# The first layer's output projection: seven block products in both pairs of columns, row sums on GpSimd

## The chip, the cores and the metric

One core of one Trainium2 chip runs the whole program. The metric is device microseconds of one execution, the median of three runs. The profile is of one more execution, whose own time and span are given below. PE is TensorE (PEld its weight load), DVE is VectorE, ACT is ScalarE, POOL is GpSimd, SP is SyncE.

## The reference

A trunk of two residual layers on 512 tokens of width 2048, all in fp32: layer 0 is gated differential attention, layer 1 is RWKV-7 time mixing. The change lies in the last product of layer 0:

```python
    out = lax.map(one_block, (jnp.arange(nb), qb))        # per head: a = p0 - lam * p1; a @ v
    ...
    o = rms_norm(o, subln_w) * (1.0 - lambda_init)
    o = o.reshape(B, T, DA_WIDTH).astype(h.dtype) * jax.nn.silu(gate)
    return o @ w_out                                      # (512, 2048) @ (2048, 2048)
...
        x = x + out.astype(x.dtype)
```

Its left operand is made head by head (8 heads of 256 columns), so its last 256 rows of K exist only when the last head's attention is done.

## The kernel before, in words

**Products.** An fp32 product is made of three matmuls of rounded halves: each operand is split into a high part and a low part, and hi x hi, hi x lo and lo x hi are added in PSUM (mm3, L123). The left operand of the output projection is the transposed result of attention, kept as 16 K tiles of 128 rows; each is a pair of tiles hH and hL of 128 x 512. The right operand is the weight, loaded 512 KB at a time (two K tiles of 512 columns) into a tile; `split_w` (L92) rounds it to wh on ACT (L105) and subtracts on DVE to get wl (L106). There are two buffers each of wh and wl.

**The projection's two units.** The output has four column blocks of 512. Blocks 0 and 1 are made one after the other by `unit_tok` (L167): 8 weight tiles for each block, 24 matmuls of 128 x 512 for each tile, summed in four PSUM banks; then DVE adds the residual x (L1100), and the result is squared on ACT (L1078) and stored. Blocks 2 and 3 are made together by `seven` (L750) in the manner of Strassen: tokens, K tiles and columns are halved, and seven block products replace eight. Sums of weight blocks are made in memory by DMAs that accumulate (`add_w`, L83), issued by POOL into the same tile that holds the first block (ropeC, ropeS, T and others). Sums of blocks of the left operand are made by `sum_forms` (L669): DVE adds hH and hL into a row buffer `frow` (L678), DVE makes the four forms S1, S3, S2, S4 in place (L687), ACT rounds each to its high half (L699), DVE subtracts for the low half (L700). With NS = 6, 12 of the 16 K tiles go through block products (three groups of 2 + 2 K tiles) and 4 K tiles (12 to 15) are plain. A weight tile in a block product feeds 12 matmuls, in a plain step 24.

**What goes beside it.** While blocks 0 and 1 are made, the attention of the last head still runs: a chain of steps (scores, exps on ACT, transposes, weighted sums, y) is stepped after every so many matmuls of the projection (`Chain`; the number is the gap, here 20, after a delay of 16). The chain for the last head writes its result straight into rows 14 and 15. For each of its four blocks of 128 queries DVE has the masked maximum (L345), the difference of the two softmax parts (L359), the low half of the transposed weights (L369), a reciprocal root by small steps (L64 to L71), y (L384) and the low halves of the transposed y (L418).

**What sets the order.** The kernel is written with tiles and priorities, and a scheduler fixes each engine's instruction order when the program is built; an engine runs its list in that order, and waits at an instruction whose input or buffer is not ready. `issue_after` adds an edge to another instruction, `high_priority` moves instructions forward in the list (splits by AHEAD, the taking of PSUM sums by SCAN). The rows of the earlier heads come from memory, where they were stored; SP loads them as hH and hL (L1055), 28 loads of 256 KB, issued up to 725.3 us.

Of the kernel before, what the change touches and what calls it, by code (L numbers as in the profile page):

```python
# [668 lines left out]
def sum_forms(g, src, i, rows, homes, halves, behind=None):  # L669
# [4 lines left out]
    for r, k0 in zip(rows, (half[i] for half in halves)):  # L674
        if isinstance(src, list):
            for k in range(KG):
                with g.tc.issue_after(g.rowsplit):
                    nc.vector.tensor_add(r[:, k], *(x[:].bitcast(F32) for x in src[k0 + k]))  # L678
# [4 lines left out]
    out = {}
    for nm, o, x, y, op in (("S1", d, b, d, ALU.subtract), ("S3", b, a, b, ALU.subtract),
                            ("S2", d, d, a, ALU.subtract), ("S4", c, c, d, ALU.add)):
        with g.tc.issue_after(behind or g.rowsplit):
            nc.vector.tensor_tensor(out=o, in0=x, in1=y, op=op)  # L687
# [201 lines left out]
def loader(g, w, homes):  # L889
# [3 lines left out]
    def load(k0, c):  # L893
# [3 lines left out]
        g.fetched = load_w(g, raw, (w, c), k0, slice(0, KG))  # L897
# [12 lines left out]
def layer0(g, aps):  # L910
    nc, tc = g.nc, g.tc
    with ExitStack() as cx:
# [137 lines left out]
        rows = []  # L1050
        for k in range(KT - 2):
            rows.append([g.hp.tile([P, T], F32R, name=n, tag=n) for n in ("hH", "hL")])
            for x, d in zip(rows[k], g.ys):
                with tc.issue_after(g.reloaded):
                    loaded = nc.sync.dma_start(out=x[:].bitcast(F32), in_=d[k * P : (k + 1) * P, :]).ins  # L1055
        ch = Chain(g, attention(g, h, *before, 20, rows, rest), 16)

        def all_rows(n, _):
            if n >= KT - 1:
                ch.finish(g)  # L1060

        yH, yL = Rows(rows, 0), Rows(rows, 1)
        g.ssx = g.const.tile([P, NT, 4], F32, name="ssx")
        g.hH, g.hL, xs = [], [], []

        def new_x(cb):
# [5 lines left out]
            return xq  # L1072
# [898 lines left out]
```

## Time and profile before

| what | number |
|---|---|
| median of 3 runs | 2050.31 us (2050.27 to 2052.22) |
| the profiled execution | 2051.32 us, its span 2049.6 us |
| granted TensorE clock | 1.000 |
| PE, DVE, ACT, POOL busy in the span | 2032.6, 1626.3, 1139.3, 409.4 us |
| output projection's first matmul | 714.15 us |
| first accumulating DMA in it (POOL) | 810.95 us |
| stretch 714.1 to 766.9 us | PE busy 52.59 of 52.80, DVE 39.12, ACT 23.83, POOL 0 |

The page gives busy time by engine, then the span in 40 slices, the DMA queues, the chain that ended last, the costliest groups of instructions. Rows of groups read: line, engine, operation, out<-in, shape, count, busy time and mean duration (ns), idle time before and what ended it. Rows of windows read: window, its length, busy time and count of PE, PEld, DVE, ACT, POOL, granted clock, DMA share, GB/s. Rows of the timeline read: start, length, engine, line, operation. Rows of waits read: who waited, for whom, microseconds in all, times, longest.

### The profile page before, as it was taken

To read this page: it belongs to the slowest core of one execution; us is meant where nothing else is said; L and a number is where in the kernel's file an instruction comes from. 1 tells how busy PE (TensorE), PEld (TensorE's weight loads), DVE (VectorE), ACT (ScalarE), POOL (GpSimd) and SP (SyncE) were. 2 spreads that over 40 slices of the span, in tenths; PEclk is the share of its full clock that TensorE was granted. 3 is DMA by queue.
4 is the path that set the end of the run, shared out by engine and by line. 5 is a ranking of instruction groups with operands and counts; after the bars stand their busy time and mean duration, and the time that the engine had idled before them with its cause. 6 is when DMAs were issued, how large, how long until landed. Compare 5 with 4: busy or idle time off the path is not lost. (4 is left out here: it accounts for less than half of the span.)

```text
span 2049.6 us, 34167 instructions
## 1 busy us (share of the span) xinstructions
PE 2032.6 (99%) x11898; PEld 1668.7 (81%) x11898; DVE 1626.3 (79%) x4126; ACT 1139.3 (56%) x2264; POOL 409.4 (20%) x786
## 2 busy tenths in 40 slices
PE   9999999999999999999999999999999999999999
PEld 8888888888888888888877788888888888877787
DVE  7988988888898977575787888877778878778865
ACT  5765656565666544355565555555555555546433
POOL 1020111102011000121122322222232222232211
PEclk9999999999999999999999999999999999999999
DMA  8487978879787965723323323233333332346796
GB/s 288 156 165 193 180 173 184 165 193 165 190 180 171 270 218 176 174 93 108 103 79 92 93 82 96 83 101 98 98 98 88 95 88 88 101 137 217 178 270 142
DMA packets 160845, 300.90 MB, mean 147 GB/s; under 512 B 64560, under 2 KB 81968, under 8 KB 160672
## 3 DMA queue, kind: packets, MB, share of 16 engines
q1 hardware_dynamic: 110416, 183.34, 28.4%
q0 software_dynamic: 26528, 92.98, 23.9%
q10 hardware_dynamic: 23728, 22.40, 3.4%
q8 instruction: 94, 1.54, 0.3%
q14 instruction: 79, 0.65, 0.1%
HBM read 274.48 MB, written 24.18 MB: 146 GB/s over the span
## 5 line engine op out<-in xcount | busy, mean ns | idle before, releaser
L106 DVE TENSOR_TENSOR wl<-wraw,wh 128x1024 fp32r<-128x1024 f32 (+1 forms) x284 | 347.5, 1224 | 155.2 <-ACT wh L105 146.1
L105 ACT CAST wh<-wraw 128x1024 fp32r<-128x1024 f32 (+1 forms) x284 | 297.4, 1047 | 232.2 <-PE pp L125 102.8
L125 PE MATMUL pp<-hL,wh 128*128 128x512 f32 x1024 | 413.5, 404 | 0.0
L125 PE MATMUL pp<-hH,wl 128*128 128x512 f32 x1024 | 413.1, 403 | 0.0
L125 PE MATMUL pp<-hH,wh 128*128 128x512 f32 x1024 | 412.3, 403 | 0.1
L125 PEld LDWEIGHTS pp<-hH,wh 128*128 128x128 f32 x1024 | 193.1, 189 | 34.5 <-ACT wh L105 0.4
L125 PEld LDWEIGHTS pp<-hL,wh 128*128 128x128 f32 x1024 | 193.1, 189 | 33.6
L125 PEld LDWEIGHTS pp<-hH,wl 128*128 128x128 f32 x1024 | 193.2, 189 | 32.5
L572 PE MATMUL pp<-wh,hH 128*128 128x512 f32 x448 | 176.8, 395 | 0.0
L572 PE MATMUL pp<-wh,hL 128*128 128x512 f32 x448 | 175.8, 393 | 0.0
L1516 DVE SCALAR_TENSOR_TENSOR tmpl<-LT,Tm 128x60 f32<-128x60 f32 (+24 forms) x496 | 135.0, 272 | 13.3
L1660 POOL COPY SA<-VS 64x64 f32<-64x64 f32 x224 | 59.4, 265 | 405.4 <-DVE VS L1676 367.4
L572 PE MATMUL pp<-wl,hH 128*128 128x512 f32 x448 | 140.2, 392 | 0.0
L125 PE MATMUL pp<-wl,hH 128*128 128x512 f32 x340 | 133.7, 393 | 0.0
L125 PE MATMUL pp<-wh,hH 128*128 128x512 f32 x340 | 133.3, 392 | 0.1
L125 PE MATMUL pp<-wh,hL 128*128 128x512 f32 x340 | 133.0, 391 | 0.1
L1518 DVE TENSOR_TENSOR Tm<-Tm,tmpl 128x60 f32<-128x60 f32 (+24 forms) x496 | 103.6, 209 | 11.7
L1657 ACT COPY rhs<-sm 64x64 f32<-64x64 f32 x256 | 53.1, 207 | 83.7 <-PE sm L1654 80.7
L572 PEld LDWEIGHTS pp<-wl,hH 128*128 128x128 f32 x448 | 84.4, 188 | 17.3
L572 PEld LDWEIGHTS pp<-wh,hH 128*128 128x128 f32 x448 | 84.2, 188 | 17.5 <-issue 0.4
L572 PEld LDWEIGHTS pp<-wh,hL 128*128 128x128 f32 x448 | 84.2, 188 | 16.0
L1667 ACT COPY VS<-sm 64x64 f32<-64x64 f32 x256 | 52.9, 206 | 75.2 <-PE sm L1665 69.2
(433 smaller groups left out, 4438.4 us busy)
## 6 DMA issues: line engine op xcount, KB each, us to landing
wraw<-in_rw_w_in_dram SPq DMA_DIRECT2D x128, 512.0 KB
wraw<-in_da_w_in_dram SPq DMA_DIRECT2D x75, 512.0 KB
wraw<-in_da_w_in_dram POOLq DMA_DIRECT2D x28, 512.0 KB, 6.6
wraw<-in_da_w_out_dram SPq DMA_DIRECT2D x26, 512.0 KB
Ta<-in_da_w_in_dram POOLq DMA_DIRECT2D x21, 512.0 KB, 5.5
Tb<-in_da_w_in_dram POOLq DMA_DIRECT2D x21, 512.0 KB, 5.7
Tc<-in_da_w_in_dram POOLq DMA_DIRECT2D x21, 512.0 KB, 5.3
Td<-in_da_w_in_dram POOLq DMA_DIRECT2D x21, 512.0 KB, 5.6
```

The lines of the kernel that those rows point to most:

```text
L105: a = nc.scalar.copy(hi[:, ks], raw[:, ks])
L106: d = nc.vector.tensor_sub(lo[:, ks], raw[:, ks], hi[:, ks].bitcast(F32))
L125: m = nc.tensor.matmul(out, a, b, start=s, stop=e, skip_group_check=skip)
L572: m = nc.tensor.matmul(out[t][:], x, wt[lo][:, k, :], start=first, stop=end and lo == 1 and k == KG - 1, skip_group_check=True)
L1516: nc.vector.scalar_tensor_tensor(tt, LT[:, i : i + 1, i + 1 :].to_broadcast([P, s, n]), n2[:, i : i + 1], Tm[:, 0:s, i : i + 1].to_broadca ...
L1518: nc.vector.tensor_add(Tm[:, 0:s, i + 1 :], Tm[:, 0:s, i + 1 :], tt)
L1657: nc.scalar.copy(rhs[r_, :], sm[r_, h * C : h * C + C])
L1660: nc.gpsimd.tensor_copy(p.SA[r_, c - 1, :], VS[r_, c, h, :])
L1667: g.copied = nc.scalar.copy(VS[r_, c, h, :], sm[r_, P : P + C])
```

## The change

Blocks 0 and 1 are now made together too, by `seven_early`, a function that the kernel already has (L812) and uses for layer 1's output projection. One step works on one weight tile. Its steps: 1 to 3 plain, K tiles 4, 10 and 12 (each with the next) for column block 0; 4 and 5 plain, 4 and 10 for block 1; then the block products on two groups of 2 + 2 K tiles (0 and 6, 2 and 8): 6 and 7 (the block called 11), 8 and 9 (12), 10 and 11 (the form S1); 12 plain; 13 and 14 (S2), 15 and 16 (S4), 17 plain, 18 and 19 (S3), 20 plain, 21 and 22 (block 22). K tiles 14 and 15, the last head's, are in the plain steps 17 and 20. Blocks 2 and 3 are made by `seven` with all 16 K tiles in block products, four groups. 

Row sums and forms are made by GpSimd (`nc.gpsimd` as `adder`), for four groups where there were three, one group's forms at a time at the steps that the table `at` names; the halves are still split by ACT and DVE. The forms' order is S1, S2, S4, S3 (also in layer 1's projection, where DVE still makes them). The rows are loaded in another order (4, 5, 10 to 13 first, then the residual of block 0, then 0, 1, 6, 7, the residual of block 1, then 2, 3, 8, 9), the weights of the first unit with the priority AHEAD, and the gap of the last head's chain is 24.

```diff
+FORMS = "S1", "S2", "S4", "S3"
+
+
+def sum_forms(g, src, i, rows, homes, halves, behind=None, names=FORMS, adder=None):
 
 
 
     nc = g.nc
...
-                with g.tc.issue_after(g.rowsplit):
-                    nc.vector.tensor_add(r[:, k], *(x[:].bitcast(F32) for x in src[k0 + k]))
+                with g.tc.issue_after(behind or g.rowsplit):
+                    (adder or nc.vector).tensor_tensor(out=r[:, k], in0=src[k0 + k][0][:].bitcast(F32),
+                                                       in1=src[k0 + k][1][:].bitcast(F32), op=ALU.add)
...
-    for nm, o, x, y, op in (("S1", d, b, d, ALU.subtract), ("S3", b, a, b, ALU.subtract),
-                            ("S2", d, d, a, ALU.subtract), ("S4", c, c, d, ALU.add)):
+    for nm, o, x, y, op in (("S1", d, b, d, ALU.subtract), ("S2", d, d, a, ALU.subtract),
+                            ("S4", c, c, d, ALU.add), ("S3", b, a, b, ALU.subtract)):
+        if nm not in names:
+            continue
         with g.tc.issue_after(behind or g.rowsplit):
-            nc.vector.tensor_tensor(out=o, in0=x, in1=y, op=op)
+            (adder or nc.vector).tensor_tensor(out=o, in0=x, in1=y, op=op)
...
-        rows = []
-        for k in range(KT - 2):
-            rows.append([g.hp.tile([P, T], F32R, name=n, tag=n) for n in ("hH", "hL")])
-            for x, d in zip(rows[k], g.ys):
-                with tc.issue_after(g.reloaded):
-                    loaded = nc.sync.dma_start(out=x[:].bitcast(F32), in_=d[k * P : (k + 1) * P, :]).ins
-        ch = Chain(g, attention(g, h, *before, 20, rows, rest), 16)
-
-        def all_rows(n, _):
-            if n >= KT - 1:
-                ch.finish(g)
-
-        yH, yL = Rows(rows, 0), Rows(rows, 1)
-        g.ssx = g.const.tile([P, NT, 4], F32, name="ssx")
-        g.hH, g.hL, xs = [], [], []
+        rows = [None] * (KT - 2)
+        halves = [0, 2, 4, 12], [6, 8, 10, 14]
+        first = [k for k0 in (4, 10, 12) for k in (k0, k0 + 1)]
+        others = [0, 1, 6, 7, 2, 3, 8, 9]
+        for k in others + first:
+            rows[k] = [g.hp.tile([P, T], F32R, name=n, tag=n) for n in ("hH", "hL")]
+        xs = []
...
+        for some, cb in ((first, 0), (others[:4], 1), (others[4:], None)):
+            for k in some:
+                for x, d in zip(rows[k], g.ys):
+                    with tc.issue_after(g.reloaded):
+                        loaded = nc.sync.dma_start(out=x[:].bitcast(F32), in_=d[k * P : (k + 1) * P, :]).ins
+            if cb is not None:
+                new_x(cb)
+        g.rowsplit = loaded
+        ch = Chain(g, attention(g, h, *before, 24, rows, rest), 16)
+
...
-        for cb in range(2):
-            pts = unit_tok(g, yH, yL, (aps["da_w_out"], cb), 512, more=(all_rows, all_sums)[cb],
-                           late=cb == 0)
-            xq = new_x(cb)
-            for t in range(NT):
-                nc.vector.tensor_add(xq[:, t, :], xq[:, t, :], pts[t][:])
-                store_x(cb, t)
...
+        at = dict(zip((1, 2, 4, 6, 8, 9, 11, 12, 13, 15, 16, 17, 18, 19, 20, 21),
+                      [(i, nm) for k in (0, 2) for nm in FORMS for i in (k, k + 1)]))
+
+        def between(n):
+            if n == 14:
+                ch.finish(g)
+            if n in at:
+                i, nm = at[n]
+                if i == len(sums):
+                    sums.append({})
+                    frow = g.work.tile([P, 2, KG, 512], F32, name="frow", tag=("sB2", "sC2", "qkT", "qkL")[i], bufs=1)
+                    frows.append([frow[:, x] for x in range(2)])
+                sums[i].update(sum_forms(g, rows, i, frows[i], homes, halves, g.m.ins, nm, nc.gpsimd))
+
...
+        load = loader(g, aps["da_w_out"], [(g.wraw, "wraw", 3)], AHEAD)
+        seven_early(g, aps["da_w_out"], load, rows, sums, 0, 1, residual(0), [flat(g.S), T2[:]], banks, stores(0),
+                    [x[:2] for x in halves], (4, 10, 12), 14, between)
...
-        seven(g, aps["da_w_out"], load, rows, sums, 2, 3, acc, [flat(g.C), flat(g.S), T2], banks, done, begin)
+        for cb in (2, 3):
+            new_x(cb)
+        T3 = g.work.tile([P, KG, 512], F32, name="T3", tag="Te", bufs=1)
+        seven(g, aps["da_w_out"], load, rows, sums, 2, 3, residual(2), [flat(g.C), T3[:], flat(g.S), T2[:]], banks,
+              stores(2), begin, halves)
```

GpSimd's list at the projection, before. The rows after the last head's weight adds are the second unit's accumulating DMAs (ropeC, ropeS and T are the tiles that hold the weight blocks):

```order
113 L86 DMA wraw<-in_da_w_in_dram 128x1024 x3
114 L86 DMA ropeC<-in_da_w_out_dram 128x1024
115 L86 DMA ropeS<-in_da_w_out_dram 128x1024
116 L86 DMA T_8533<-in_da_w_out_dram 128x1024
117 L86 DMA ropeC<-in_da_w_out_dram 128x1024
```

And now, at the same place (L680 the row sums, L692 the forms, T_7653 the tile T2):

```order
113 L86 DMA wraw<-in_da_w_in_dram 128x1024 x3
114 L680 TENSOR_TENSOR frow<-hH,hL 128x512 x4
115 L692 TENSOR_TENSOR frow<-frow 128x2x256 x4
116 L680 TENSOR_TENSOR frow<-hH,hL 128x512 x4
117 L692 TENSOR_TENSOR frow<-frow 128x2x256 x4
118 L86 DMA ropeS<-in_da_w_out_dram 128x1024
119 L680 TENSOR_TENSOR frow<-hH,hL 128x512 x5
120 L692 TENSOR_TENSOR frow<-frow 128x2x256
121 L680 TENSOR_TENSOR frow<-hH,hL 128x512
122 L692 TENSOR_TENSOR frow<-frow 128x2x256
123 L86 DMA T_7653<-in_da_w_out_dram 128x1024
```

The sums of the first two groups stand ahead of the first accumulating DMA, and eight sums of the third group stand between that DMA and the next.

ACT's list in the second block of the last head's attention, before (L368 the high half of the transposed weights, L351 the exps, L105 the fifth weight tile's cast):

```order
697 L368 CAST at<-pt 128x128
698 L351 ACTIVATE a,sm<-sc,nb,sq 128x256
699 L351 ACTIVATE sc,sm<-sc,nb,sq 128x256
700 L105 CAST wh<-wraw 128x1024
701 L378 ACTIVATE o,so<-o,r 128x256
```

And now, where L707 are the casts of GpSimd's forms:

```order
697 L707 CAST fS_7694<-frow 128x512
698 L707 CAST fS_8255<-frow 128x512
699 L368 CAST at<-pt 128x128
700 L707 CAST fS_7926<-frow 128x512
701 L707 CAST fS_8183<-frow 128x512
702 L105 CAST wh<-wraw 128x1024
703 L351 ACTIVATE a,sm<-sc,nb,sq 128x256
704 L351 ACTIVATE sc,sm<-sc,nb,sq 128x256
```

Two casts of the first group stand ahead of the transposed weights, two more ahead of the fifth weight tile's cast.

DVE's list around step 7 (the split of tile T2, L106), which has in it the accumulations into the residual (L748), the low halves of forms (L708) and attention's steps:

```order
1669 L748 TENSOR_TENSOR xq<-xq,pp 128x512
1670 L69 SCALAR_TENSOR_TENSOR rs_t<-rs_t,so 128x1
1671 L348 SCALAR_TENSOR_TENSOR nb<-mx,sq 128x1
1672 L106 TENSOR_TENSOR wl<-T_7653,wh 128x1024
1673 L71 SCALAR_TENSOR_TENSOR ro<-rs_t,rs_i 128x1
1674 L708 TENSOR_TENSOR fS_8206<-frow,fS_8205 128x512
1675 L382 SCALAR_TENSOR_TENSOR ro<-ro,r,stats_107 128x1
1676 L708 TENSOR_TENSOR fS_8522<-frow,fS_8522 128x512
1677 L384 SCALAR_TENSOR_TENSOR y<-o,ro,G 128x256
```

Before, no L678, L687 or L700 row of this projection and no accumulation into the residual stood among attention's rows.

More of the change, by code (lines that the diff above doesn't have):

```diff
@@ L747, in pieces, with seven @@
     return prod, plain, take
-def seven(g, w, load, rows, sums, c1, c2, acc, Ts, banks, done, begin=None, halves=evenly(NS)):
+def seven(g, w, load, rows, sums, c1, c2, acc, Ts, banks, done, begin=None, halves=None):
     prod, plain_, take = pieces(g, load, rows, sums, acc, halves)
@@ L896, in load @@
         raw = pool.tile([P, KG, 512], F32, name="wraw", tag=tag, bufs=bufs)
-        g.fetched = load_w(g, raw, (w, c), k0, slice(0, KG))
+        with g.tc.high_priority(offset=offset):
+            g.fetched = load_w(g, raw, (w, c), k0, slice(0, KG))
         return raw
@@ L1071, in new_x @@
             xs.append(xq)
-            return xq
+        for some, cb in ((first, 0), (others[:4], 1), (others[4:], None)):
[7 more added lines that the diff above has]
+        ch = Chain(g, attention(g, h, *before, 24, rows, rest), 16)
+        g.ssx = g.const.tile([P, NT, 4], F32, name="ssx")
+        g.hH, g.hL = [], []
         def store_x(cb, t):
@@ L1083, in layer0 @@
                              for t in tags]
-        homes = ({"S1": one("dd0H", "dd0L"), "S2": one("VL"), "S4": one("t1", "t1"), "S3": one("t1", "t1")},
-                 {"S1": one("Td"), "S2": one("sA2"), "S4": one("acc1"), "S3": one("Ta")},
-                 {"S1": one("at", "al"), "S2": one("sC2"), "S4": one("dd1H", "dd1L"),
-                  "S3": one("Tc")})
-        def all_sums(n, _):
-            if n >= 4 * len(sums) + 2 and len(sums) < NS // KG:
-                frow = g.work.tile([P, 2, KG, 512], F32, name="frow", tag=("qkT", "qkL")[len(sums) % 2],
-                                   bufs=1)
-                sums.append(sum_forms(g, rows, len(sums), [frow[:, i] for i in range(2)], homes, evenly(NS)))
@@ L1095, in layer0 @@
[L1095 to L1108 removed]
+        halved = {}
@@ new lines, in half_of, with home @@
+        def half_of(tag):
+            def home():
+                if tag not in halved:
+                    both = g.work.tile([P, 2, 2, KG, 256], F32R, name="f" + tag, tag=tag, bufs=1)
+                    halved[tag] = [both[:, 0], both[:, 1]]
+                return halved[tag].pop(0)
+            return home
+        homes = ({"S1": one("dd0H", "dd0L"), "S2": one("Ta"), "S4": one("acc1"), "S3": one("dd1H", "dd1L")},
+                 {"S1": one("Td"), "S2": half_of("sA2"), "S4": one("t1", "t1"), "S3": one("t1", "t1")},
+                 {"S1": one("at", "al"), "S2": one("VL"), "S4": half_of("sC2"), "S3": one("Tc")},
+                 {"S1": half_of("sA2"), "S2": half_of("sB2"), "S4": half_of("sB2"), "S3": half_of("sC2")})
@@ L1110, in banks, with residual, stores, done @@
+        def residual(c0):
+            return {nm: [xs[c0 + c][:, 2 * t + i, :] for i in range(2)] for nm, (t, c) in PLACES.items()}
+        def stores(c0):
+            def done(nm):
+                t, c = PLACES[nm]
+                for i in range(2):
+                    store_x(c0 + c, 2 * t + i)
+            return done
         def banks(i):
```

22 lines of the change are left out of this document (8 added, 14 removed).

## The prediction

> **What bounds the kernel now.** I read the head of the page first, then the stretch of the output projection (714 to 893 us of the span) in windows, then its waits, its groups of instructions, and single rows of the timeline.
>
> ```profile
> PE 2032.6 (99%) x11898; PEld 1668.7 (81%) x11898; DVE 1626.3 (79%) x4126; ACT 1139.3 (56%) x2264; POOL 409.4 (20%) x786
> ```
> ```profile
> 740.00:750.00 10.00, 9.93 (x55) 7.91 (x53) 8.24 (x33) 5.67 (x14) 0.00 (x0) 1.00 0.43 155
> 750.00:760.00 10.00, 9.88 (x54) 8.04 (x52) 6.40 (x30) 4.75 (x11) 0.00 (x0) 1.00 0.33 99
> 770.00:780.00 10.00, 10.00 (x46) 8.29 (x45) 9.93 (x15) 6.62 (x15) 0.00 (x0) 1.00 0.57 187
> 780.00:790.00 10.00, 10.00 (x45) 8.29 (x45) 9.92 (x16) 4.24 (x6) 0.00 (x0) 1.00 0.37 123
> 860.00:870.00 10.00, 10.00 (x46) 8.29 (x45) 5.80 (x6) 4.04 (x4) 3.20 (x4) 1.00 1.05 195
> ```
> The columns are length, busy time of PE, PEld, DVE, ACT and POOL, granted clock, DMA share, GB/s. PE is the bound: no gap, full clock. So matmuls that go are gained, unless something else then arrives late. DVE is almost full at 770 to 790, where it makes the row sums, but that is no bound: PE beside it has no gap. What one matmul is worth is read from start to start, not from its busy time (0.39 us, overlapped with the next):
>
> ```profile
> 870.28 0.39 PE L125 MATMUL pp<-wh,fS 128*128 128x512 f32 x1
> 870.50 0.39 PE L125 MATMUL z<-wh,hH 128*128 128x512 f32 x1
> 870.73 0.39 PE L125 MATMUL z<-wl,hH 128*128 128x512 f32 x1
> 870.96 0.39 PE L125 MATMUL z<-wh,hL 128*128 128x512 f32 x1
> ```
> That is 0.227 us each (0.68 us for three). Last, who waits there:
>
> ```profile
> POOL ropeC L86 <- DVE wl L106: 156.6, 3, 133.8
> ACT wh L105 <- PE pp L125: 45.3, 26, 4.4
> DVE wl L106 <- ACT wh L105: 41.4, 26, 4.2
> PE z L125 <- DVE wl L106: 0.2, 1, 0.2
> ```
> POOL does nothing for 133.8 us up to its first accumulating DMA; ACT and DVE wait for buffers that PE frees, up to 4.4 us. PE's own longest wait is 0.2 us.
>
> **The change, part by part.** *Matmuls.* A plain pair of columns costs 384 matmuls (16 K tiles, 4 row tiles, 2 columns, 3 each). Each pair of K tiles in block products saves 6. Before: 384 for the first unit, 384 - 6x6 = 348 for the second. Now 384 - 4x6 = 360 and 384 - 8x6 = 336. So 732 become 696: 36 fewer, 36 x 0.227 = **8.2 us gained** if nothing is late.
>
> *DVE.* It loses the row sums and forms, and gains splits and accumulations:
>
> ```profile
> L687 DVE TENSOR_TENSOR frow<-frow 128x512 f32<-128x512 f32 x12 | 8.3, 688 | 0.1
> L678 DVE TENSOR_TENSOR frow<-hH,hL 128x512 f32<-128x512 f32 x12 | 7.7, 686 | 0.0
> L700 DVE TENSOR_TENSOR fS<-frow,fS 128x512 fp32r<-128x512 f32 x12 | 8.1, 687 | 0.7 <-ACT fS L699 0.7
> L699 ACT CAST fS<-frow 128x512 fp32r<-128x512 f32 x12 | 7.1, 618 | 9.1 <-DVE frow L687 9.0
> L1100 DVE TENSOR_TENSOR xq<-xq,pp 128x512 f32<-128x512 f32 x8 | 5.1, 684 | 1.2 <-PE pp L125 1.2
> L106 DVE TENSOR_TENSOR wl<-wraw,wh 128x1024 fp32r<-128x1024 f32 x33 | 40.4, 1224 | 23.3 <-ACT wh L105 23.2
> L105 ACT CAST wh<-wraw 128x1024 fp32r<-128x1024 f32 x33 | 34.7, 1052 | 35.9 <-PE pp L125 27.8 <-DVE xq L745 4.4 <-PE pp L572 1.6
> ```
> Gone: 24 x 0.687 = 16.5 us. Added: 4 more low halves (2.7 us), and the accumulations into the residual, 28 + 16 where there were 8 + 20, so 16 x 0.684 = 10.9 us. Over the projection DVE is 2.9 us lighter, which is worth nothing in itself. What counts is the place. Before, all of it came after attention, at 764 to 830. Now accumulations and low halves stand between the steps of the last head's attention, on the same in-order DVE, and from step 6 each weight tile feeds 12 matmuls (2.7 us) instead of 24 (5.4 us), so splits come twice as often. Each tile's split (L106) must be done before PE may begin its step.
>
> ```profile
> 735.36 1.23 DVE L106 TENSOR_TENSOR wl<-wraw,wh 128x1024 fp32r<-128x1024 f32 x1
> ```
> ```profile
> 736.50:766.89 30.39, 30.19 (x152) 24.42 (x151) 23.20 (x93) 12.58 (x29) 0.00 (x0) 1.00 0.48 166
> ```
> ```profile
> L106 DVE TENSOR_TENSOR wl<-wraw,wh 128x1024 fp32r<-128x1024 f32 x5 | 6.1, 1224 | 0.0
> L678 DVE TENSOR_TENSOR frow<-hH,hL 128x512 f32<-128x512 f32 x3 | 2.0, 684 | 0.0
> L379 DVE TENSOR_SCALAR so<-so 128x1 f32<-128x1 f32 x4 | 0.6, 150 | 3.4 <-ACT o L378 3.4
> L355 DVE RECIPROCAL r<-sm 128x2 f32<-128x2 f32 x2 | 0.3, 161 | 1.0 <-ACT sc L351 1.0
> ```
> The split of the fifth tile ends at about 736.5. In the 30.4 us behind it DVE is busy 23.2, of which 6.1 and 2.0 are splits and row adds (the first two rows below it, of the same window): 15.1 us are attention's. In the new order there stand, behind the fifth split up to and with that of step 11: 6 splits (7.3 us), 8 accumulations (5.5), 7 low halves (4.8) and some 15 us of attention, together 32.6. So the split of step 11 ends at 736.5 + 32.6 = 769.1 at the earliest. When does PE want it? Ahead of step 11 stand 5 x 24 + 5 x 12 = 180 matmuls of the projection:
>
> ```profile
> 714.10:766.90 52.80, 43.81 (x180) 32.88 (x180) 0.69 (x1) 0.00 (x0) 1.00 0.69 233
> ```
> ```profile
> 748.69 0.36 PE L125 MATMUL o<-V,at 128*128 128x256 f32 x1
> 748.88 0.28 PE L125 MATMUL o<-VL,at 128*128 128x256 f32 x1
> ```
> The first row is the projection's matmuls alone: PE had issued 180 by 766.9. In the new order 12 narrow ones of attention (0.19 apart by the other two rows) and four transposes (about 0.1 each, an estimate) come only later, so PE would be there at about 764.2. DVE makes it 769.1 - 764.2 = **4.9 us late**, and PE cannot win that back. Some of DVE's waits stay as well: behind 736.5 it waits 3.4 us for attention's squares (L379) and 1.0 for the exps now; work that fills most of that gap leaves me 0.8 us (my choice between 0 and 4.4).
>
> *GpSimd's adds.* Of a two-input add there no row exists. Nearest rows:
>
> ```profile
> L1568 POOL COPY G<-AR 64x512 f32<-64x512 f32 x24 | 17.2, 715 | 93.1 <-PE px L1561 92.4
> L1480 POOL TENSOR_SCALAR_AFFINE_SELECT G<-G 64x1024 f32<-64x1024 f32 x32 | 37.2, 1161 | 1.0
> ```
> ```profile
> 882.53 8.48 POOL L1126 TENSOR_SCALAR xq<-xq,rs 128x512 f32<-128x512 f32 x4 [13.74 <-DVE rs L71]
> 900.30 6.46 POOL L1126 TENSOR_SCALAR xq<-xq,rs 128x512 f32<-128x512 f32 x4 [9.30 <-DVE rs L71]
> ```
> A copy of 512 elements takes 0.72 us, a pass over 1024 takes 1.16, a multiplication of 512 by a row's scale 1.6 to 2.1. An add reads twice 512, so I take 1.2, with 0.72 and 2.12 as ends. [...] No run here shows it yet.
>
> Two places hang on it. First: the four row adds and four forms of the first group need rows that are loaded last but for four.
>
> ```profile
> 725.26 0.38 SPq L1055 DMA_DIRECT2D hL<-ys  x1
> ```
> ```profile
> 720.00:730.00 10.00, 9.98 (x50) 7.99 (x50) 6.84 (x24) 5.66 (x14) 0.00 (x0) 1.00 0.99 337
> 745.71 0.39 PE L125 MATMUL sc<-qkT,qkL 128*128 128x512 f32 x1
> ```
> The loads of rows are issued up to 725.3 with the DMA full (0.99), and I put the first group's last row at 728 (an estimate). One row add and four forms follow: 728 + 5 x 1.2 = 734. The last cast (0.62) then stands ahead of the fifth tile's cast (1.05) on ACT and its split (1.22): 736.9, against 736.5. Nothing. Second: the third group's buffer is that of the last head's q and k, free after PE's last scores: 745.7 before, and some 1.5 later now, since DVE's first lateness falls ahead of it. Eight GpSimd instructions lie between that and the form S3 of that group, whose cast (ACT) and low half (DVE) stand ahead of attention's and of the splits of steps 8 to 11: 747.2 + 9.6 + 0.6 = 757.4, where DVE by its own sum comes at 755.9. That is **1.5 us**. At 0.72 it is nothing; at 2.12 the first place costs 5 and the second 9.
>
> *DMA.* The accumulating loads go from 12 to 24, 16 of them in the second unit.
>
> ```profile
> q0 software_dynamic: 1728, 6.29, 38.7%
> q1 hardware_dynamic: 1749, 5.41, 17.9%
> ```
> From 800 to 893 us: 12 adds of 512 KB took 38.7% of 93 us, 3.0 us of all engines each; a plain load 1.6. The second unit (336 x 0.227 = 76 us) asks for 16 x 3.0 + 12 x 1.6 = 67 us, with stores and residual some 13 more: just full. An add has at least one round of four tiles (10.9 us) to land. I take 0.5 us, between 0 and 4.
>
> *Same cost before and after*: reordered row loads and the other order of the forms in layer 1's projection (nothing late there: PE is full).
>
> **Sum**: -8.2 + 4.9 + 0.8 + 1.5 + 0.5 = **-0.5 us** on the profiled execution, 2051.3 (span 2049.6 and 1.7 around it). That one lies 1.0 above the median of 2050.3, so the forecast is 2050.8 there and 2049.8 for a median.
>
> **Rivals.** *All is hidden.* DVE's extra work in attention fits into its gaps, GpSimd's into its idle time. For it: PE waits for nobody now, DVE idles 7.2 of 30.4 us, POOL altogether. Against it: 32.6 us of DVE rows in some 28. It gives -8.2: 2042.
>
> *The GpSimd adds decide (slower).* At 1.7 us the fifth tile's cast comes 2.9 us late, the third group's S3 another 5.5: -8.2 + 4.9 + 0.8 + 2.9 + 5.5 + 0.5 = +6.4, 2056.7. It decides from about 1.55 us. For it: the multiplication rows; against it: the pass over 1024.
>
> *DVE and GpSimd keep each other out (slower).* While DVE was busy 9.32 of 10 us the four multiplications took 8.48 us, later 6.46: something makes GpSimd slower beside a busy DVE.
>
> ```profile
> 880.00:890.00 10.00, 9.82 (x43) 7.76 (x42) 9.32 (x17) 5.74 (x9) 7.47 (x4) 1.00 0.31 113
> ```
> DVE's own splits kept 1.22 us. If each of the 13 low halves and splits behind 736.5 had to wait out half an add (0.6), DVE would be 7.8 us later: +7.3, 2057. [...]
>
> *The second unit is bound by its adds.* The queue of 80 us of transfers in 76 costs 4 us instead of 0.5: +3, 2053. For it 1.05 in the window at 860 with three tiles a round; against it, PE has no gap there.
>
> **How the numbers follow.** Chances: forecast 0.39, all hidden 0.25, slow adds 0.18, keeping out 0.07, adds in the second unit 0.11. A measurement of this kernel can tell about 0.2%, 4.1 us. Faster by more: all hidden, and a tenth of the forecast's, 0.29. Same: most of the forecast, two thirds of the last rival, a little of the slow adds, 0.43. Slower: the rest, 0.28. The forecast's own range is 2046.5 to 2053 (add at 0.72, to 1.4 us). The range that holds 8 in 10 reaches from all hidden to slow adds: 2041.5 to 2057.5.
>
> **What would show it.** Matmuls of the projection: 696, and the end of the projection moved by less than 8.2 us. GpSimd's add rows near 1.2 us. In the windows from 740 to 775, DVE over 9.5 of 10, and PE gaps there of some 7 us in all, ended by splits (L106) that end late; before 736 none. In the second unit hardly a gap. I am wrong if DVE has idle time in that stretch, if PE's gaps name casts of GpSimd's forms from step 4 on, or if PE has no gaps.

## The result and the profile after

The changed kernel is slower: 2071.64 us (median; 2068.87 to 2073.44) against 2051.26 us (2050.27 to 2052.77) for the kernel before on the same chip, a ratio of 1.0093 with an interval of 1.0078 to 1.0108. The forecast was 2049.8, its range ended at 2057.5. The profiled execution, the longest of the four, has a span of 2071.7 us where the kernel before had 2049.6: 22.1 us to be found.

Where are they? The mark I use is GpSimd's first causal mask in layer 1, which both kernels come to 60 us after the projection. Of its six instructions the group's row names the start of the first; the first row is of the kernel before, the second of the changed one.

```profile
L1478 POOL TENSOR_SCALAR_AFFINE_SELECT G<-G x6: 654/656/690, 953.7 to 1066.7; 64x512 f32<-64x512 f32 x6
```
```profile
L1509 POOL TENSOR_SCALAR_AFFINE_SELECT G<-G x6: 653/654/658, 968.6 to 1080.9; 64x512 f32<-64x512 f32 x6
```

So 14.9 us are lost by then, 7.2 later. The projection's own end moved by the same 14.9: the first matmul behind it (`lora`) starts at 908.6 us, before at 893.7. The head of the page, then the four largest of PE's waits between 720 and 910 us, then windows of 10 us there:

```profile
PE 2035.1 (98%) x11862; PEld 1669.1 (81%) x11862; DVE 1651.6 (80%) x4131; ACT 1151.1 (56%) x2277; POOL 468.3 (23%) x830
```
```profile
PE pt L365 <- DVE rs_i L65: 5.6, 1, 5.6
PE pp L125 <- DVE wl L106: 3.4, 1, 3.4
PE pt L297 <- ACT t L282: 2.5, 1, 2.5
PE z L125 <- DVE wl L106: 2.3, 2, 1.7
```
```profile
720.00:730.00 10.00, 7.54 (x31) 5.89 (x30) 7.20 (x20) 3.94 (x11) 4.94 (x4) 0.83 0.92 319
740.00:750.00 10.00, 4.38 (x17) 3.73 (x16) 9.39 (x20) 2.81 (x9) 7.98 (x6) 0.86 0.69 255
760.00:770.00 10.00, 6.02 (x23) 4.32 (x23) 10.00 (x17) 3.12 (x6) 9.97 (x8) 0.88 0.07 13
800.00:810.00 10.00, 8.30 (x28) 5.85 (x27) 8.81 (x8) 5.44 (x7) 7.17 (x6) 0.83 0.74 147
860.00:870.00 10.00, 10.00 (x46) 8.29 (x45) 5.73 (x6) 3.74 (x4) 3.21 (x4) 1.00 1.06 202
```

The matmuls are gone as counted: 11862 against 11898, 36 fewer. But PE, whose longest wait in the projection before was 0.2 us, now has four long ones in the first unit. All eight rows of that view add to 16.2 us. And the granted clock is below 1 there: the windows from 720 to 810 that lie below 1 lack 0.17, 0.14, 0.03, 0.12, 0.05 and 0.17, times 10 us makes 6.8 us. So -8.2 + 16.2 + 6.8 = 14.8, against 14.9 measured. (The sum is that good in part by luck: two of the slow stretches begin inside a gap, so some 0.4 us is counted twice.) In the second unit (the last row) PE is full beside a DMA share of 1.06.

What happens in such a gap is seen in the timeline at the first of them.

```profile
721.35 4.43 POOL L680 TENSOR_TENSOR frow<-hH,hL 128x512 f32<-128x512 f32 x3 [44.52 <-DMA hL<-ys]
723.09 1.24 DVE L348 SCALAR_TENSOR_TENSOR nb<-mx,sq 128x1 f32<-128x1 f32 x1
724.59 1.22 DVE L278 TENSOR_TENSOR rr<-rr,stats 128x8 f32<-128x8 f32 x1
725.84 1.28 ACT L282 ACTIVATE t<-t,rr 128x128 f32<-128x128 f32 x4 [0.93 <-DVE rr L278]
726.29 0.76 PE L297 MATMUL pt<-ident,t 128*128 128x128 f32 x2 [2.46 <-ACT t L282]
727.28 0.63 PE L125 MATMUL pp<-wh,hL 128*128 128x512 f32 x1
727.71 0.63 PE L125 MATMUL pp<-wh,hH 128*128 128x512 f32 x1
```

GpSimd makes three row sums in a row. Beside them two DVE instructions on one and eight columns take 1.2 us each, about as long as a GpSimd sum. The second is an input of ACT's scaling, that of PE's transpose, and PE stands still for 2.46 us. Then its matmuls start 0.43 us apart where 0.227 is usual, for 3.4 us (the granted clock from 726.4 to 729.8 us was 0.53). The shortest gap of the change with a slow stretch behind it is this one:

```profile
804.29 0.50 PE L125 MATMUL z<-wl,fS 128*128 128x512 f32 x1 [1.70 <-DVE wl L106]
```

That these DVE instructions are stretched, and which are not, is read from groups by shape, 715 to 775 us; first the kernel before, then the changed one.

```profile
L106 DVE TENSOR_TENSOR wl<-wraw,wh 128x1024 fp32r<-128x1024 f32 x9 | 11.0, 1223 | 1.6 <-ACT wh L105 1.6
L348 DVE SCALAR_TENSOR_TENSOR nb<-mx,sq 128x1 f32<-128x1 f32 x8 | 1.2, 157 | 0.1
L345 DVE CUSTOM_DVE_ANT_0 sc<-sc,mask 128x512 f32<-128x512 f32 x2 | 1.4, 696 | 0.0
```
```profile
L106 DVE TENSOR_TENSOR wl<-wraw,wh 128x1024 fp32r<-128x1024 f32 x6 | 8.6, 1433 | 4.6 <-ACT wh L105 4.6
L348 DVE SCALAR_TENSOR_TENSOR nb<-mx,sq 128x1 f32<-128x1 f32 x8 | 3.2, 411 | 0.0
L345 DVE CUSTOM_DVE_ANT_0 sc<-sc,mask 128x512 f32<-128x512 f32 x2 | 1.4, 686 | 0.0
L748 DVE TENSOR_TENSOR xq<-xq,pp 128x512 f32<-128x512 f32 x10 | 6.6, 675 | 0.3 <-PE pp L125 0.3
```

Stretched in these groups are those with two inputs in SBUF (nb from mx and sq: 157 to 411 ns in the mean; splits 1.22 to 1.43). Those with one input in PSUM keep their time (L345 with the scores: 696 and 686 ns; L748 with pp: 675, where the accumulation L1100 before took 684). GpSimd's own sums, in groups from 700 to 900 us, and one of the shortest, for which DVE waited and not the other way round:

```profile
L692 POOL TENSOR_TENSOR frow<-frow 128x512 f32<-128x512 f32 x16 | 25.6, 1597 | 9.5 <-DVE fS L708 4.8 <-DVE so L379 3.3 <-DVE fsA L708 0.6
L680 POOL TENSOR_TENSOR frow<-hH,hL 128x512 f32<-128x512 f32 x16 | 22.5, 1444 | 49.7 <-DMA hL<-ys 48.2 <-PE sc L125 1.4
```
```profile
764.43 1.26 POOL L692 TENSOR_TENSOR frow<-frow 128x512 f32<-128x512 f32 x1
```

The second loss is in layer 1's projection, where DVE still makes the forms and only their order has changed. First a row of the kernel before, then three of the changed one and its window.

```profile
1898.26 1.42 DVE L687 TENSOR_TENSOR frow<-frow 128x512 f32<-128x512 f32 x2 [0.16 <-DMA frow<-yd]
```
```profile
1903.78 0.77 POOL L665 DMA_DIRECT2D frow<-yd  x1 [2.94 <-ACT fS L707]
1912.90 1.42 DVE L692 TENSOR_TENSOR frow<-frow 128x512 f32<-128x512 f32 x2 [3.34 <-DMA frow<-yd]
1914.97 0.77 PE L1685 MATMUL sm<-VS,G 128*128 128x128 f32 x2 [2.54 <-DVE VS L1707]
1910.00:1920.00 10.00, 7.46 (x27) 5.98 (x27) 4.88 (x8) 3.42 (x9) 0.91 (x3) 0.72 0.29 100
```

The form S3 overwrites the first half of the row buffer, and it is made last now, so the buffer comes free later; the load of the next rows goes out late, DVE waits 3.34 us for it, and behind DVE's waiting instruction stands VS, a step of the recurrent scan, which PE needs. PE stops for 2.54 us and then runs at half speed for 6.8 us (the clock from 1914.5 to 1921.3 was 0.50, in the window of 10 us it is 0.72): 2.54 of gap and half of 6.8 make some 6 us, most of the 7.2.

### The profile page after: what moved, and what is told of

Read it like the earlier page. It is cut to its first block, busy times and chain, and to the rows that moved or that the text cites. A ratio compares the mean times of both kernels' runs of the same rounds, so it can differ in the third digit from the quotient of the medians.

```text
span 2071.7 us, 34196 instructions
## 1 busy us (share of the span) xinstructions
PE 2035.1 (98%) x11862; PEld 1669.1 (81%) x11862; DVE 1651.6 (80%) x4131; ACT 1151.1 (56%) x2277; POOL 468.3 (23%) x830
## 4 chain that ended last, share of the span: by engine, by line
PE 82%; DVE 8%; issue 4%; ACT 3%; DMA 2%; POOL 1%; SPq 0%; POOLq 0%; ACTq 0%; DVEq 0%
PE pp L125 40%; PE pp L572 24%; PE pt L125 2%; DVE wl L106 2%; PE gp L1488 2%; PE sm L1685 1%; PE z L125 1%; PE o L125 1%; PE sc L125 1%; PE sm L1703 1%; PE sm L1696 1%; ACT wh L105 1%; PE Y L1725 1%; DMA T<-in_rw_w_out_dram 1%; PE pt L297 1%
## 5 line engine op out<-in xcount | busy, mean ns | idle before, releaser
L106 DVE TENSOR_TENSOR wl<-wraw,wh 128x1024 fp32r<-128x1024 f32 (+1 forms) x281 | 345.7, 1230 | 155.3 <-ACT wh L105 146.2
L105 ACT CAST wh<-wraw 128x1024 fp32r<-128x1024 f32 (+1 forms) x281 | 294.2, 1047 | 225.4 <-PE pp L125 98.6
L572 PE MATMUL pp<-wh,hH 128*128 128x512 f32 x448 | 176.8, 395 | 0.0
L572 PE MATMUL pp<-wh,hL 128*128 128x512 f32 x448 | 175.8, 392 | 0.0
L1547 DVE SCALAR_TENSOR_TENSOR tmpl<-LT,Tm 128x60 f32<-128x60 f32 (+24 forms) x496 | 135.0, 272 | 13.2
L572 PE MATMUL pp<-wl,hH 128*128 128x512 f32 x448 | 140.2, 392 | 0.0
L125 PE MATMUL pp<-wl,hH 128*128 128x512 f32 x272 | 109.9, 404 | 3.9 <-DVE wl L106 3.9
L125 PE MATMUL pp<-wh,hH 128*128 128x512 f32 x272 | 107.9, 398 | 1.4 <-DVE mixE L1315 0.8
L125 PE MATMUL pp<-wh,hL 128*128 128x512 f32 x272 | 108.7, 400 | 0.0
```

What stands on the lines that cost most here:

```text
L105: a = nc.scalar.copy(hi[:, ks], raw[:, ks])
L106: d = nc.vector.tensor_sub(lo[:, ks], raw[:, ks], hi[:, ks].bitcast(F32))
L125: m = nc.tensor.matmul(out, a, b, start=s, stop=e, skip_group_check=skip)
L572: m = nc.tensor.matmul(out[t][:], x, wt[lo][:, k, :], start=first, stop=end and lo == 1 and k == KG - 1, skip_group_check=True)
L1547: nc.vector.scalar_tensor_tensor(tt, LT[:, i : i + 1, i + 1 :].to_broadcast([P, s, n]), n2[:, i : i + 1], Tm[:, 0:s, i : i + 1].to_broadca ...
```

## The experiments

My theory after reading the trace had two parts. **A**: while GpSimd reads SBUF, DVE's instructions with two SBUF inputs wait for it (and it for them: its sums took 1.44 and 1.60 us in the mean, 1.26 at the shortest), the chain of small DVE steps in attention grows long, and PE waits; **A2**: the new order of forms costs the 7 us in layer 1. The rivals: **B**, ACT and DVE wait in order for GpSimd's slow chain of sums; **C**, DVE is overloaded among attention's steps, whoever makes the sums (the prediction's own 4.9 us).

The table has medians (e3 stands apart, below), their ratio to the kernel before as run beside them, and the start of layer 1's first mask in the profiled execution, relative to the 953.7 us of the kernel before. A profiled execution need not lie near its median: those of the change, e1, e6 and e8 are the longest of their runs, those of e4, e7 and e11 the shortest, by up to 3.3 us. So medians and marks are compared each with their own kind.

| run | median, us | ratio to before (interval) | first mask |
|---|---|---|---|
| the change | 2071.64 | 1.0093 (1.0078 to 1.0108) | +14.9 |
| e1, old order of forms in layer 1 | 2065.63 | 1.0059 (1.0044 to 1.0074) | +16.1 |
| e2, before, with idle adds on GpSimd | 2067.72 | 1.0067 (1.0050 to 1.0084) | +14.7 |
| e4, e1 with sums that read nothing | 2049.36 | 0.9984 (0.9974 to 0.9993) | -3.7 |
| e5, before, with idle writes on GpSimd | 2051.90 | 1.0001 (0.9992 to 1.0010) | +0.3 |
| e6, e1 with sums on DVE | 2058.76 | 1.0037 (1.0023 to 1.0050) | +8.8 |
| e7, before, all K tiles in the second unit | 2051.42 | 0.9999 (0.9990 to 1.0008) | -2.0 |
| e8, before, its sums on GpSimd after attention | 2071.45 | 1.0095 (1.0081 to 1.0109) | +19.6 |
| e9, e1 with copies of a column and writes | 2057.85 | 1.0023 (1.0013 to 1.0033) | +4.5 |
| e10, one group, sums on DVE | 2054.40 | 1.0013 (1.0003 to 1.0023) | +2.5 |
| e11, sums on DVE, no waits for loads | 2046.33 | 0.9975 (0.9965 to 0.9985) | -5.9 |

### e1: layer 1 keeps its old order of forms

```diff
+    forms = (("S1", ...), ("S2", ...), ("S4", ...), ("S3", ...))
+    for j in range(4) if isinstance(src, list) else (0, 3, 1, 2):
+        nm, o, x, y, op = forms[j]
```

> The changed kernel, with the forms of layer 1's projection made in the old order (S1, S3, S2, S4) again; layer 0 as changed. In the changed kernel's profile the first landmark behind layer 0's projection is 14.9 us late against before, the end 22 us: some 7 us go in layer 1, around a 2.5 us wait of PE at 1915 us, where DVE waits 3.3 us for a row load. Theory A (the new order of the forms holds the row buffer longer, so its next load comes late, and DVE's scan step stands behind it): 5 to 7 us come back, 2065 to 2067 us. Theory B (layer 1 is late only because its start is shifted against DMA traffic): no change, 2070 to 2073.

2065.63 us, 6.0 less than the change by the medians, and 7.2 less when each is taken against the kernel before of its own series (13.2 over it against 20.4). The wait for VS is down to 0.3 us in PE's waits there, and the mark behind the first projection did not come earlier, so the gain is layer 1's alone. A2 holds.

### e2: the kernel before, with adds on GpSimd that nobody waits for

```diff
+        spare = ...
+        for i in range(26):
+            with tc.issue_after(loaded):
+                nc.gpsimd.tensor_tensor(out=spare[:, i // 2 % 2, i % 2], in0=rows[i % 14][0][:].bitcast(F32),
+                                        in1=rows[i % 14][1][:].bitcast(F32), op=ALU.add)
```

> The kernel before, with 26 GpSimd adds of 128x512 (row hH + row hL into a spare tile that nobody reads) put beside the last head's attention, from the moment the rows are loaded; nothing waits for them, the order on PE, DVE and ACT is the old one. Theory A (a GpSimd add and a DVE instruction with two SBUF inputs keep each other out): DVE's small steps stretch from 0.16 to over 1 us, PE gets gaps, the time goes up by 3 to 15 us, 2054 to 2066. Theory B (the changed kernel is slow because its casts, splits and products wait for slow GpSimd sums in the lists): nothing waits for these adds, so no change, 2050 to 2052.

This is the main test: PE, DVE, ACT and SP have the same instructions in the same order as in the kernel before; only GpSimd adds rows into a tile that nobody reads. It costs 15.3 us, at the upper end of what I had put down, and its mark is as late as the change's (+14.7 and +14.9). No instruction waits for these adds. PE's longest waits, the DVE groups and GpSimd's group:

```profile
PE pt L297 <- ACT t L282: 6.2, 1, 6.2
PE o L125 <- DVE y L384: 3.5, 1, 3.5
```
```profile
L106 DVE TENSOR_TENSOR wl<-wraw,wh 128x1024 fp32r<-128x1024 f32 x7 | 9.9, 1415 | 3.2 <-ACT wh L105 3.2
L348 DVE SCALAR_TENSOR_TENSOR nb<-mx,sq 128x1 f32<-128x1 f32 x8 | 3.5, 461 | 0.0
L1060 POOL TENSOR_TENSOR spare<-hH,hL 128x512 f32<-128x512 f32 x25 | 35.3, 1426 | 16.8 <-DMA hL<-ys 16.1
730.00:740.00 10.00, 8.85 (x29) 7.12 (x30) 5.51 (x8) 3.48 (x7) 9.69 (x8) 0.64 0.53 181
```

The stretched instructions are those of the change (L348 at 461 ns), and the clock falls behind PE's gap (0.64 in the window). A is shown, without B or C.

### e3 and e5: writes in place of the adds

e3 had three memsets for each of e2's adds:

> As the run with 26 GpSimd adds beside the old kernel's attention, but each add is replaced by three GpSimd memsets of the same tile (some 0.5 us each), which write SBUF and read nothing. Theory A (it is the reading of SBUF that keeps DVE out): no change, 2050 to 2052, DVE's steps keep 0.16 us. Theory C (any GpSimd work beside DVE costs): about as slow as with the adds, 2054 or more.

It tells nothing on A: with no input to wait for, GpSimd made them early, at 678 to 716 us, and the executions fell into two groups, three between 2050.7 and 2053.9 us and seven between 2071 and 2078. The profile is of one of the first group. The mean granted clock of the seven is 0.994 to 0.996, that of the three 0.999 to 1.000, which are the values of the change (0.995), where PE has gaps, and of the kernel before (1.000); where the seven lose their 20 us no profile shows. e5 ties the writes to the rows, so that they run where e2's adds did:

```diff
...
+                nc.gpsimd.tensor_copy(spare[:, i // 2 % 2, i % 2, 0:1], rows[i % 14][1][:, 0:1].bitcast(F32))
+                for _ in range(2):
+                    nc.gpsimd.memset(spare[:, i // 2 % 2, i % 2], 0.0)
```

> The kernel before with GpSimd work that writes only, this time in the same stretch as the 26 adds were: each add is replaced by a copy of one column of the loaded row (which keeps the wait) and two memsets of 128x512. (In the first run of this kind the memsets waited for nothing and ran ahead of the stretch, and its executions fell into two groups, 2051 to 2054 and 2071 to 2078, which is not understood.) Theory A (only reading SBUF keeps DVE out): 2050 to 2054, DVE's small steps at 0.16 us but for those beside a copy. Theory C (any GpSimd work beside DVE costs): 2058 or more.

1.0001 (0.9992 to 1.0010): no cost, and L348 back at 155 ns.

```profile
L348 DVE SCALAR_TENSOR_TENSOR nb<-mx,sq 128x1 f32<-128x1 f32 x8 | 1.2, 155 | 0.1
```

So in this stretch it is what the adds read from SBUF that keeps DVE out, not GpSimd's being busy (33 us more than in the kernel before, from 698 to 745 us; in e2 36 us more, from 697 to 751) and not its writing. How much of it a read with one input would do was not tried. That writing is free in other places is not shown: e3's 20 us are unexplained.

### e4 and e9: the change, with GpSimd's reading taken out

e4 replaces each sum by three memsets and a copy of one column (its output leaves out the sums).

> The changed kernel with layer 1's old form order, where each GpSimd add and form is replaced by three memsets of the same region (about as long, 1.5 us) and, for a row add, a copy of one column that keeps the wait for the loaded row: left out are the sums of blocks of the left operand (zeros in their place). Theory A (mutual exclusion with DVE costs most): close to what the sum of the prediction gave without it, 2046 to 2053. Theory B (the length of the GpSimd chain in front of ACT's casts costs most): 2060 to 2067. Some rows of DVE's and ACT's lists stand elsewhere than in the changed kernel, since memsets are planned otherwise.

16 us less than e1, the mark 3.7 us earlier than before. But most memsets wait for nothing and ran ahead, so that B was taken away along with A. e9 puts the waits back: the copied columns are taken from what the sums read, one for a row sum, two for a form, and two memsets follow (like e4, it leaves out the sums).

```diff
...
-            (adder or nc.vector).tensor_tensor(out=o, in0=x, in1=y, op=op)
...
+                nc.gpsimd.tensor_copy(o[:, 0, 0:1], x[:, 1, 255:256])
+                nc.gpsimd.tensor_copy(o[:, 1, 0:1], y[:, 0, 255:256])
+                for _ in range(2):
+                    nc.gpsimd.memset(o, 0.0)
```

> The kernel of the experiment with layer 1's old order of forms, and in it each of GpSimd's sums is replaced by a copy of one column (two for a form), which reads what the sum read and so has its waits, and by two memsets of 512 columns, which write what the sum wrote; the sums themselves, and so the right values of the forms, are left out of its output. GpSimd's chain thus stays about as long (some 1.2 us a sum) and the lists of the engines nearly as they are, but GpSimd hardly reads SBUF. Theory A (reading by GpSimd keeps DVE's two-input instructions out): the 14 to 16 us go, 2046 to 2053, and DVE's 128x1 instructions in the first unit stay at 0.16 us. Theory B (it is the length of GpSimd's chain, for which ACT and DVE wait in order): 2058 or more, with ACT's casts of fS and PE behind them waiting as before.

2057.85, between the two theories and nearer to B's 2058 than to A's 2053; the mark is at +4.5, e1's at +16.1, e4's at -3.7. The 128x1 instructions are at their old time, but PE waits for casts on ACT, 4.1 us in three waits:

```profile
L348 DVE SCALAR_TENSOR_TENSOR nb<-mx,sq 128x1 f32<-128x1 f32 x8 | 1.1, 153 | 0.0
PE pp L125 <- ACT wh L105: 2.4, 2, 1.9
PE z L125 <- ACT wh L105: 1.7, 1, 1.7
```

Of the 19.8 us between the marks of e1 and e4, 11.6 went with the reading (A) and 8.2 with the wait for the chain (B). By the medians, 2065.63, 2057.85 and 2049.36, it is 7.8 and 8.5. So both are real, and which is the larger is not shown. Nor is the division clean: the schedules of the three differ, and e9's copies of one column take 0.53 and 0.44 us in the mean for the forms, where those for the row sums take 0.21.

### e6, e10 and e11: the sums on DVE

e6 makes all sums on DVE, in e1's order (`sum_forms` without its `adder`).

> The changed kernel with layer 1's old form order and with the row sums and forms of layer 0's projection on DVE instead of GpSimd. Theory A (mutual exclusion is the loss): the 32 sums cost DVE 0.69 us each, 22 us, some 13 of them among attention; with splits already 4.9 us late by the count of DVE's rows that gives 8 to 14 us of lateness and no exclusion: 2052 to 2058, faster than with GpSimd (2065.6). Theory D (GpSimd relieves DVE, and the loss is elsewhere): slower than 2065.6.

2058.76, just above A's range: 7 us less than on GpSimd, 6.7 more than the kernel before. By its size this looked like C, and I took it so at first. The trace says otherwise: from 740 to 790 DVE is busy 9.65 to 10 of 10 us and PE loses 0.4 us in all. What PE waits for is elsewhere, and behind it DVE waits for loads:

```profile
PE pp L125 <- DVE wl L106: 9.1, 2, 8.2
PE pt L297 <- ACT t L282: 2.9, 1, 2.9
723.63 0.69 DVE L680 TENSOR_TENSOR frow<-hH,hL 128x512 f32<-128x512 f32 x1 [2.20 <-DMA hL<-ys]
817.04 8.21 SPq L1068 DMA_DIRECT2D xq<-in_x_dram  x8
832.99 1.33 DVE L750 TENSOR_TENSOR xq<-xq,pp 128x512 f32<-128x512 f32 x2 [9.04 <-DMA xq<-in_x_dram]
```

The residual of blocks 2 and 3 goes into the row buffers of the third and fourth group, which come free only with their last form, at 817 us; and the very first row sum stands on DVE ahead of attention before its row has come.

e10 tried one group instead of two in the first unit, with the sums on DVE (24 matmuls fewer):

```diff
...
-        first = [k for k0 in (4, 10, 12) for k in (k0, k0 + 1)]
+        first = [k for k0 in (4, 10, 8) for k in (k0, k0 + 1)]
...
-                    [x[:2] for x in halves], (4, 10, 12), 14, between)
+                    [x[:1] for x in halves], (4, 10, 8, 2, 12), 14, between)
```

> The change with layer 1's old order of forms, with all sums on DVE, and with only one of the four groups of K tiles in block products in the first unit: 24 matmuls fewer than the kernel before instead of 36, -5.4 us, and nothing on GpSimd. Ahead of the end of attention stand then 9 plain steps of 24 matmuls (49 us), so that a split is wanted every 5.4 us there, and the sums of one group only (8 x 0.69 us). Theory A (GpSimd's reading and DVE's overload among attention were the whole loss): DVE's rows behind 736 shrink to about what there is time for, 2045 to 2051. Rival (any order in which sums and splits stand among attention loses more than 24 matmuls bring): 2053 to 2058, with PE waiting for splits between 740 and 775.

2054.40, just above the kernel before (2052.46). The rival held in the number and not in the place: between 740 and 780 PE is nearly full, and it waits for splits between 785 and 815, where sums and low halves stand on DVE ahead of them.

```profile
PE pp L125 <- DVE wl L106: 2.7, 3, 1.2
PE z L125 <- DVE wl L106: 1.4, 1, 1.4
800.00:810.00 10.00, 7.52 (x31) 5.14 (x29) 6.04 (x9) 5.42 (x9) 0.00 (x0) 1.00 0.65 193
```

e11 takes e6 and works against its two waits for loads, by the steps of the sums, by making the third group's forms ahead of the fourth's, and by which buffer holds which residual:

```diff
...
-tag=("sA", "sB", "qkL", "qkT")[cb]
+tag=("sA", "sB", "qkT", "qkL")[cb]
...
-        at = dict(zip((1, 2, 4, 6, 8, 9, 11, 12, 13, 15, 16, 17, 18, 19, 20, 21),
-                      [(i, nm) for k in (0, 2) for nm in FORMS for i in (k, k + 1)]))
+        at = dict(zip((2, 3, 4, 6, 8, 9, 11, 12, 13, 14, 15, 16, 17, 18, 19, 20),
+                      [(i, nm) for nm in FORMS for i in (0, 1)] + [(i, nm) for i in (2, 3) for nm in FORMS]))
```

> The version with all sums on DVE and layer 1's old order of forms, with three changes against its two waits for loads: the first group's sums begin a step later (behind the row that DVE waited 2.2 us for, with 2.9 us lost by PE), the third group's forms are made ahead of the fourth's, not in turn with them, and the residual of block 2, which is needed first, goes into the third group's row buffer, block 3's into the fourth's (DVE waited 9.0 us for a residual that could only be loaded from 817 us on, with 8.2 us lost by PE). Theory A (in the version with sums on DVE these two waits, with the slow clock behind each, were the whole loss, and DVE's full list among attention costs nearly nothing): 36 matmuls less come through, the projection ends 5 to 9 us earlier than in the kernel before, 2043 to 2048. Theory B (the prediction's 4.9 us of DVE lateness is there too, and only hid behind the other waits): 2048 to 2053, with PE waiting for splits between 740 and 775.

2046.33 (2043.38 to 2049.29) against 2051.57: a ratio of 0.9975, 0.9965 to 0.9985, faster than both kernels. By the medians that is 5.2 us. The profiled execution, the shortest of nine (2043.38), has a span of 2041.5, 8.1 us less than the profiled one before; but only 5.9 of them are there at the mark, the rest comes in layer 1, and no run explains it. In the projection -8.2 for 36 matmuls and 2.8 us more of PE's waits (3.5 against 0.7 from 700 to 910 us) make -5.4. The wait for the first row has shrunk from 2.20 to 1.23 us, the wait for the residual is gone. The stretch from 740 to 780 in one window, PE's longest wait, the issue of the residuals, block 2's now at 804, and the split of step 11:

```profile
740.00:780.00 40.00, 39.27 (x193) 32.92 (x193) 39.09 (x110) 20.95 (x40) 5.12 (x6) 1.00 0.70 169
PE pt L297 <- ACT t L282: 1.9, 1, 1.9
804.39 2.37 SPq L1068 DMA_DIRECT2D xq<-in_x_dram  x4
765.43 1.22 DVE L106 TENSOR_TENSOR wl<-T,wh 128x1024 fp32r<-128x1024 f32 x1
```

DVE is busy 39.09 of 40 us, and PE 39.27. C is refuted as a loss of some 5 us between 740 and 780: here a full DVE is not a late one.

### e7: only the second unit's part of the change

The kernel before with all 16 K tiles in block products in the second unit, sums on DVE: 12 matmuls fewer.

> The kernel before with only the second unit changed: all 16 K tiles in block products (four groups), the sums on DVE, behind attention; the first unit plain as before. 12 matmuls fewer, 12 x 0.227 = 2.7 us, 8 more row sums and forms and 4 more low halves on DVE (8.2 us) in a stretch where it idles at 800 to 810. If that is hidden and the 16 accumulating DMAs do not bind: 2049 to 2050.5 where the kernel before has 2052.4. If the accumulating DMAs bind the second unit: 2053 to 2056.

0.9999 (0.9990 to 1.0008). The span of the profiled execution, the shortest of eleven, is 2.7 us less, as 12 x 0.227 says, but the executions spread from 2048.57 to 2054.12, and the medians show no gain. What takes the 2.7 us in most of them stays open; in the profiled one PE is full beside the four additional accumulating loads (10.00 of 10 us at a DMA share of 1.05, 860 to 870 us).

### e8: GpSimd's sums, held back until attention is done

The kernel before, with its 24 sums on GpSimd and a copied column ahead of the first two groups that ties them to row 15:

> The kernel before, its row sums and forms (12 and 12) on GpSimd instead of DVE, but held back until the last head's attention is done (copies of one column of the last row's low half stand ahead of them). DVE there only has splits and accumulations, and PE needs the sums 45 us later. Theory A (mutual exclusion costs time only where PE waits for DVE's next result): DVE's splits stretch to 2 us in places, PE has no gap, 2051 to 2054. Rival: exclusion costs wherever it occurs: 2058 or more.

I had expected this to be nearly free, since attention's chain of small steps is over by then. It was as slow as the change itself. Two rows of it, PE's longest wait and what DVE did just before:

```profile
PE pp L125 <- DVE xq L1104: 6.5, 1, 6.5
775.67 1.09 DVE L701 TENSOR_TENSOR fS<-frow,fS 128x512 fp32r<-128x512 f32 x1 [6.73 <-ACT fS L700]
```

A low half (L701) stands on DVE ahead of the accumulations (L1104) that free PE's banks, and waits 6.73 us for a cast that waits for GpSimd. This is B: slow sums that others stand behind, in lists whose order was fixed ahead. A is in it too: two of DVE's splits beside the sums take 1.85 and 2.28 us where 1.22 is usual.

## Why the prediction was wrong, point by point

The step that failed in the first unit: the sum has a term for when DVE's rows come and one for the length of GpSimd's adds, but none for what an add does to the DVE instruction beside it. That stood only as a rival. The runs showed it in the place of the 4.9 us: e2 loses 15 us by it alone. The second step that failed is the order of layer 1's forms, put at nothing and worth 6 to 7 us. The terms of 0.8 and 1.5 us no run isolates.

- **36 matmuls: right in number.** The count is 11862. That they are worth 8.2 us fits e11, whose projection ends 5.9 us earlier with 2.8 us more of waits; its whole span, 8.1 shorter, has 2.2 us in it that came in layer 1.
- **DVE 4.9 us late at the split of step 11: wrong.** In e11 DVE is nearly as full as I said (39.09 of 40 us), yet PE's gaps there are 0.7 us, and that split ends at 766.65 instead of 769.1 at the earliest, with eight sums ahead of it on DVE that I had not counted there. The error is in attention's share: the 15.1 us stand for the 85 rows of a window of the old kernel, but behind the fifth split and ahead of that of step 11 come some 66 of attention's rows in the changed kernel and 59 in e11. The rest comes later. Full need not be late.
- **Rival "DVE and GpSimd keep each other out": the right mechanism, at a chance of 0.07 and too low a price.** I held against it that splits kept 1.22 us beside GpSimd's multiplications, where GpSimd lost time (8.48 us for four, later 6.46). Beside the 32 sums they took up to 2.29. Why the four multiplications did not hold DVE's splits up no run shows; a multiplication reads one full tile, an add two. What the traces show is that adds cost 15.3 us (e2), writes and copies of one column nothing (e5, 1.0001), and that L348 goes from 157 to 411 ns beside the sums while L345 and L748 keep their time. An instruction with one SBUF input was stretched too, once: L276 took 1.25 us in e2, 0.16 in e5.
- **Its price was +7.3 by 13 stretched splits and low halves.** Between the fifth split and that of step 11 these 13, counted rightly, took 15.8 us instead of 12.1, some 0.28 more a row where my estimate was 0.6. The costlier ones are the tiny ones: ten 128x1 rows in the same stretch took 8.9 us where 1.7 is usual, and attention has a chain of them behind which PE's transposes stand. That is why gaps come at 723 to 726 as well, where I said there would be none. The signs that I had named nearly came all the same (from 740 to 780 DVE busy 9.39 to 10.00 of 10 us, PE idle for 10.4): they could not tell a list that is too long from rows that are stretched.
- **Not priced at all: the clock behind a gap.** Matmuls at 0.43 us instead of 0.227 for 3.4 us at a time, 6.8 us over the first unit. The clock granted within these stretches was 0.50 to 0.53. Gaps of 1.70, 2.46 and 2.54 us were enough, while one of 1.92 (in e11) was not; no run shows what decides.
- **GpSimd's add at 1.2 us: right at its shortest (1.26), wrong in the mean (1.44 and 1.60).** The rival of slow adds was to decide from 1.55. In the traces it is mixed with the exclusion; e9 puts the waiting in order at some 8 us, roughly.
- **Layer 1's other order of forms at nothing: wrong, 6.0 us by the medians, 7.2 against the kernels before.** "PE is full" says nothing on what becomes late when a buffer comes free later. The step to look at was the load that waits for S3.
- **Second unit: 0.5 us, and the rival of +3: right to be small, by the profile.** PE is busy 10.00 of 10 at a DMA share of 1.06.
- **The rival "all is hidden", 2042: the change with sums on DVE and its loads in order comes to 2046.33 by the median and 2043.4 in its best execution.** Most of the work can be hidden, as this rival had it, but on DVE and not on the engine that the change chose.

## What to carry to other kernels

An idle GpSimd was not free capacity here beside a busy DVE (e2's 26 adds, for which nothing waits, cost 15.3 us): before moving elementwise work to it, count DVE's instructions with two SBUF inputs in the same stretch, the 128x1 ones first, and ask whether a chain of them leads to PE. When a forecast says that an in-order engine is overloaded, look at which rows of the new list wait for loads and buffers; with the sums on DVE two such waits held PE for 11.1 us, and shortening them moved the median from 2058.76 to 2046.33 us. A gap of PE of some 2 us is to be priced with the slow clock that may come behind it: here 3.4 us at half speed behind gaps of 1.70 and 2.46 us, 6.8 behind one of 2.54, none behind one of 1.92.

## What the runs showed of the hardware that I had not expected

- A DVE instruction of 128x1 elements took 1.24 us beside GpSimd's adds (0.16 alone), about the length of one such add (1.26 at its shortest). Three stretched ones whose end can be set beside that of a sum end with it: L278 at 725.81 us (the sums at 725.78), L69 at 765.71 (765.69), L71 at 769.15 (769.13).
- Memsets and copies of one column on GpSimd in the same place cost nothing (ratio 1.0001), adds cost 15.3 us (e2).
- Behind gaps of PE matmuls of 512 columns start 0.43 us apart. In the change's profile these stretches last 3.4 us (behind 1.70, 2.46, 3.36 and 5.62 us of gap) or 6.8 (behind 2.54); behind a gap of 1.92 us in e11 there was none.
- e3, whose memsets ran at 678 to 716 us, had executions in two groups 20 us apart. That stays open.
